# Four modulation vectors of a hybrid encoder layer: summed beside the branch merge instead of in the delta-rule stage, two of them straight into columns

## The chip, the cores and the metric

The kernel runs on one core of one Trainium2 chip. The core has five engines that run at once, each through an instruction list of its own, in order: PE (TensorE, matrix products, with its weight loads listed apart as PEld), DVE (VectorE), ACT (ScalarE), POOL (GpSimd) and SP (SyncE, which here issues nearly all DMA transfers). They wait for one another through semaphores. The metric is the device time of one execution in microseconds (us), as the median of several runs. All data is float32. Large products are made from operands split into a high part and a remainder of a reduced format ("fp32r"), three products for one.

## The reference, cut to what matters

One layer over 1024 tokens of width 1024. A conditioning vector c gives six vectors of 1024 numbers; the first two modulate the input, the last four are those of this change.

```
mod = silu(c) @ w_ada + b_ada                 # 1024 x 6144 matrix, once
shift_t, scale_t, gate_t, shift_f, scale_f, gate_f = split(mod, 6)
h = x * (1 + scale_t) + shift_t
proj = h @ w_in
o_a = gated_deltanet(...)                     # 8 heads, chunks, delta rule
o_b = chunk_band_attention(...)               # 16 heads
merged = sigmoid(gates_a) * (o_a @ w_branch_a) + sigmoid(gates_b) * (o_b @ w_branch_b)
x = layernorm(alpha * x + gate_t * (merged @ w_o), ln1_g, ln1_b)
h = x * (1 + scale_f) + shift_f
u = causal_dwconv(h @ w_up) + b
x = layernorm(alpha * x + gate_f * ((silu(u_gate) * u_val) @ w_down), ln2_g, ln2_b)
```

gate_t is needed first after the merge, shift_f and scale_f right after it in the first layer norm, gate_f only near the end.

## The kernel before, in words

The work runs through these stages; tokens lie along rows or columns of 128-wide tiles.

- **Head** (to about 95 us): the first two modulation vectors, x transposed and modulated, written as a high part `hh` and a remainder `hl`.
- **Delta-rule stage** (to about 860 us, its last chain to 920): for each of 8 heads the projections (`halves`, L281), convolutions, a triangular solve on DVE (L660, L662), an inverse by small matrix products (L684 on), and a chain over 8 chunks (L720 on). Between the heads PE is filled with projections of the merge gates (`gate_block`). Here, two calls a head, sits `mod_rows` (L800 to L823): a column block of 512 of the last four vectors is summed on DVE. Each of its four transfers brings 128 x 2 x 512 numbers (512 KB) of `w_ada` into a buffer `raw` (L808); DVE multiplies each half by a number per partition and adds it to a sum (L813 the first, L815 the other seven). PE then adds the 128 partitions with one product against a tile of ones (L819), DVE adds the bias (L822), and the row goes to `mod_d` in DRAM (L823). Eight blocks, 32 transfers, 64 DVE operations. Sum and row live in the two buffers of the ring `gt`, which the gate projections also use to store their results.
- **Attention** (about 780 to 1342 us), 16 heads. Its last heads overlap with the next stage.
- **Merge** (about 1253 to 1455 us): for branch A (`br` 0) and B (`br` 1) and each j of 8, `wblock` loads a block of 128 columns of `w_branch` into `raw`, ACT casts it to `wh` (L174), POOL takes the remainder `wl` (L177), and PE runs 48 products of 512 columns (L1039). At j = 5 to 7 of branch A, branch B's input is loaded and split the same way (ACT, DVE); in branch B the output weights `wo` are.
- **Mix** (about 1455 to 1550 us): the product with `w_o` (L1103), first layer norm, x transposed and modulated (L1155) with columns `g1f` and `b1f`. shift_f and scale_f come back from `mod_d` as 16 rows (L1110), are transposed on PE (L1112) and turned into those columns by four small DVE operations (L1116 to L1119). gate_t comes back as a broadcast tile `gtb`.
- **Up, down, last norm** (to the end).

Two things set the order around the change. First, a scheduler writes each engine's list before the run, from a simulated timeline and priorities; on the chip each engine follows its list whatever comes ready. Second, buffers are handed on in the order of the program text: `raw` has three buffers, taken in turn by every `wblock`, every split load and every `w_ada` transfer, and a transfer into one waits until the one three places earlier in the text has been used up. The slot called B4 holds, in attention, part of the transposed probabilities (the group "X", only for groups of query tiles with more than 8 blocks); after attention the group "M" lies there, from which the ring `macc` is cut.

```
    "phx": _at("X", 512, 2), "plx": _at("X", 512, 2, 256),
    ...
    group("X", _E1[4], 1024, F32R)
    ...
    group("M", _E1[4], 1024)
```

Of the kernel before, what the change touches and what calls it, by code (L numbers as in the profile page):

```python
# [9 lines left out]
F32 = mybir.dt.float32  # L10
F32R = mybir.dt.float32r
AF = mybir.ActivationFunctionType
ALU = mybir.AluOpType
# [4 lines left out]
P = 128  # L18
S = 1024
D = 1024  # L20
NK = 8
# [16 lines left out]
RB = 3  # L38
# [35 lines left out]
def _at(group, step_, n, first=0):  # L74
    return tuple((group, first + step_ * i) for i in range(n))
# [26 lines left out]
    "bt": _at("GA", 640, 2), "sb": (*_at("GA", 640, 4, 1280), ("FA", 384)),  # L102
    "ot": (("GA", 3840), ("FA", 0)), "mx": _at("FA", 4, 8, 256),

    "gb": _at("GB", 512, 2), "macc": _at("M", 0, 1), 
    "st": _at("ST", 12, 2), "mv": _at("ST", 4, 4, 36), "gtb": (_E1[0],), "g1b": (_E1[1],),
    "b1b": (_E1[2],), "r": (_E1[3], ("GL", 0)), "x1": _at("GL", 1024, 2, 1024),
    "h2": _at("GL", 0, 1, 3072),
# [42 lines left out]
def hybrid_layer(  # L151
# [69 lines left out]
    def nm(s):  # L221
        uid[0] += 1
        return f"{s}_{uid[0]}"
# [34 lines left out]
    def ring(key, shape, dtype=F32):  # L258
        return place(step(key, AT[key]), shape, dtype, key)
# [5 lines left out]
    def mtile(name, tag="m"):  # L265
        return pbank(name, tag)
# [531 lines left out]
    macc = [None]  # L798

    def mod_rows(i):  # L800

        cb = i // 2
        if i % 2 == 0:
            macc[0] = ring("gt", [P, 512])
        acc = macc[0]
        for k0 in range(4 * (i % 2), 4 * (i % 2) + 4, 2):
            rv = W.tile([P, 2, 512], F32, tag="raw", bufs=RB, name=nm("raw"))
            SP.dma_start(rv, w_ada2[k0 * P:(k0 + 2) * P,  # L808
                                    2 * D + 512 * cb:2 * D + 512 * cb + 512].rearrange(
                                        "(k p) n -> p k n", p=P))  # L810
            for k in (k0, k0 + 1):
                if k == 0:
                    DVE.tensor_scalar(acc, rv[:, 0, :], csil[:, 0:1], None, ALU.mult)  # L813
                else:
                    DVE.scalar_tensor_tensor(acc, rv[:, k - k0, :], csil[:, k:k + 1], acc,  # L815
                                             ALU.mult, ALU.add)
        if i % 2 == 1:
            pr_ = mtile(nm("pmod"), "i")
            PE.matmul(pr_, ones, acc, start=True, stop=True)  # L819
            row = ring("gt", [P, 512])[0:1, :]  # L820
            SP.dma_start(row, b_ada[:, 2 * D + 512 * cb:2 * D + 512 * cb + 512])
            DVE.tensor_tensor(row, row, pr_[0:1, :], ALU.add)  # L822
            SP.dma_start(mod_d[:, 512 * cb:512 * cb + 512], row)  # L823

    gate_block(0)
    cs = [stage_k(0)]
    gates = iter([*range(1, 2 * NK), *((i,) for i in EP)])
# [9 lines left out]
    for h in range(HA):  # L837
        ORD = "sigKq"
        for o in ORD:
            if o == "s":  # L840
                with tc.high_priority(offset=PF):
                    stage_solve(h, cs[h])
            elif o == "i":
                with tc.high_priority(offset=PI):
                    stage_inverse(h, cs[h])
            elif o == "K" and h + 1 < HA:
                with tc.issue_after(last.ins) if last else nullcontext():
                    cs.append(stage_k(h + 1))
            elif o == "g":
                some_gates(GA[h])  # L850
            elif o == "q" and h + 1 < HA:
                stage_q(h + 1, cs[h + 1])
        some_gates(GB[h])
        for i in (2 * h, 2 * h + 1):
            mod_rows(i)
        if h + 1 < HA:
            stage_vz(h + 1, cs[h + 1])
        with tc.high_priority(offset=PC):
            stage_chain(h, cs[h])
        with tc.high_priority(offset=PT):  # L860
            stage_out(h, cs[h])
        last = cs[h]["last"]
# [160 lines left out]
    for k in range(NK):  # L1023
        load_split(oahk[k], oalk[k], oa_d[k], ACT, POOL if k in OL else DVE)

    wo = []
    for br in range(2):
        if br == 1:
            mh, ml = (t_.rearrange("p k s -> p (k s)").rearrange("p (t k q) -> p t k q", t=NT, k=NK)
                      for t_ in (hh, hl))  # L1030
        rh, rl = ((oahk, oalk), (obh, obl))[br]
        for j in range(NK):
            w = wblock(kview(wbr[br], j * P, P), NK)
            for n in range(2):
                N = slice(512 * n, 512 * n + 512)
                ps = pbank(nm("pbr"), "ab"[br])
                for k in range(NK):
                    for a, r in ((w[0], rh), (w[0], rl), (w[1], rh)):
                        PE.matmul(ps, a[:, k, :], r[k][:, N],  # L1039
                                  start=(k == 0 and a is w[0] and r is rh),  # L1040
                                  stop=(k == NK - 1 and a is w[1]))
# [70 lines left out]
    PE.transpose(pmr[:, 0:16], mrow, ident[0:16, 0:16])  # L1112
    aff = cst.tile([P, 24], F32, tag="aff", name="aff")
    g1f, b1f, s1 = aff[:, 0:8], aff[:, 8:16], aff[:, 16:24]
    g1c, b1c = vt[:, VO["ln1g"]:VO["ln1g"] + 8], vt[:, VO["ln1b"]:VO["ln1b"] + 8]
    DVE.tensor_scalar(s1, pmr[:, 8:16], 1.0, None, ALU.add)  # L1116
    DVE.tensor_tensor(g1f, s1, g1c, ALU.mult)
    DVE.tensor_tensor(b1f, s1, b1c, ALU.mult)
    DVE.tensor_tensor(b1f, pmr[:, 0:8], b1f, ALU.add)  # L1119
    late, t2f = [], []  # L1120
    group("TE", "FT", 1024)
    group("TO", "B4", 1024)
# [454 lines left out]
```

## Time and profile before

| | |
|---|---|
| median of 3 runs | 2288.16 us (2286.59 to 2290.62) |
| the profiled execution | 2286.11 us |
| its span, first to last instruction | 2284.4 us |
| PE, DVE, ACT, POOL busy in the span | 94%, 71%, 45%, 34% |
| mean granted clock of PE | 0.975 |
| DMA | 220.49 MB, 97 GB/s on average |

The profile gives one execution. A group's line reads: line of the kernel, engine, operation, output and inputs by tile name, shapes, count, then busy microseconds and the mean of one in nanoseconds, then the time that the engine stood idle before these instructions and what released it. A row of the timeline reads: start, length, engine, line, operation, count, and in brackets the idle time ahead of it with its releaser. In the timeline a matrix product is shown with its modelled length; products overlap, so the pace of PE is read from one start to the next. SPq is SP's list of transfers; its lengths are those of the issue, not of the transfer.

### The profile page before, as it was taken

How to read it: one execution, taken by the hardware profiler on the slowest of the kernel's cores; microseconds unless marked ns; L12 is line 12 of the kernel's file. 1: busy time of each engine (PE TensorE's matmuls, PEld its weight loads, DVE VectorE, ACT ScalarE, POOL GpSimd, SP SyncE). 2: the span in 40 equal slices, each digit the busy share in tenths (PEclk: the TensorE clock that was granted, in tenths of full speed). 3: DMA queues.
4: the chain of work that ended last, by engine and by line, in shares of the span. 5: the costliest groups of instructions: out<-in, count | busy, mean ns of one | idle time of the engine just before them, and what ended most of it. 6: DMA issues, size and time to landing. Idle time of an engine off the chain costs nothing. (4 is left out here: it accounts for less than half of the span.)

```text
span 2284.4 us, 31690 instructions
## 1 busy us (share of the span) xinstructions
PE 2144.3 (94%) x11469; PEld 1787.2 (78%) x11469; DVE 1619.3 (71%) x3194; ACT 1026.9 (45%) x2193; POOL 772.1 (34%) x653
## 2 busy tenths in 40 slices
PE   6999999999999999999999999997999999978887
PEld 5777788777877888898897888885888888866675
DVE  8468576675757754768667434479988888789988
ACT  4645343442424335667666432244544444453322
POOL 4323233222332323233433314152100000279674
PEclk9999999999999999999999999998999999989998
DMA  9232333323333312211114333421322222333232
GB/s 280 84 108 69 106 91 106 106 72 107 99 105 107 100 41 98 63 59 49 59 55 140 103 120 106 134 93 65 102 83 83 83 84 83 111 129 111 74 111 83
DMA packets 227265, 220.49 MB, mean 97 GB/s; under 512 B 27355, under 2 KB 184468, under 8 KB 227108
## 3 DMA queue, kind: packets, MB, share of 16 engines
q1 hardware_dynamic: 227027, 218.44, 30.2%
q8 instruction: 90, 1.47, 0.3%
q14 instruction: 68, 0.55, 0.1%
q10 hardware_dynamic: 80, 0.03, 0.0%
HBM read 177.48 MB, written 47.23 MB: 98 GB/s over the span
## 5 line engine op out<-in xcount | busy, mean ns | idle before, releaser
L177 POOL TENSOR_TENSOR wl<-raw,wh 128x1024 fp32r<-128x1024 f32 x88 | 212.3, 2414 | 328.3 <-ACT wh L174 284.9
L1278 PE MATMUL pup<-hh,wop 128*128 128x512 f32 x704 | 228.8, 396 | 6.0 <-ACT SB L1291 4.0
L1278 PE MATMUL pup<-t,wop 128*128 128x512 f32 x792 | 190.1, 393 | 3.9 <-DVE t L177 2.5
L1278 PEld LDWEIGHTS pup<-t,wop 128*128 128x128 f32 x792 | 148.6, 188 | 37.9 <-DVE t L177 2.8
L1278 PEld LDWEIGHTS pup<-hh,wop 128*128 128x128 f32 x704 | 134.9, 192 | 35.7 <-ACT SB L1291 4.4
L1319 POOL TENSOR_TENSOR cc<-cc,G 128x512 f32<-128x512 f32 x22 | 36.8, 1671 | 362.5 <-DVE G L1301 313.3
L174 ACT CAST wh<-raw 128x1024 fp32r<-128x1024 f32 x88 | 92.4, 1050 | 139.5 <-DMA raw<-in_w_in_dram 55.9
L281 PE MATMUL pqkv<-hh,wh 128*128 128x512 f32 x352 | 142.8, 406 | 0.0
L281 PE MATMUL pqkv<-hl,wh 128*128 128x512 f32 x352 | 140.7, 400 | 0.0
L1278 PE MATMUL pup<-hl,wop 128*128 128x512 f32 x352 | 139.8, 397 | 0.8 <-DVE hl L177 0.8
L281 PE MATMUL pqkv<-hh,wl 128*128 128x512 f32 x352 | 139.5, 398 | 0.0
L1461 PE MATMUL pdn<-dop,dop 128*128 128x512 f32 x480 | 121.8, 412 | 18.5 <-DVE dop L177 8.6
L660 DVE TENSOR_TENSOR FT<-FT,G 128x16 f32<-128x16 f32 (+30 forms) x248 | 120.8, 487 | 18.2 <-POOL G L605 10.9
L941 POOL TENSOR_SCALAR G<-G,FT 128x640 f32<-128x640 f32 (+4 forms) x103 | 70.3, 685 | 182.3 <-DVE FT L940 161.3
L1461 PEld LDWEIGHTS pdn<-dop,dop 128*128 128x128 f32 x480 | 94.0, 198 | 43.9 <-DVE dop L177 9.7
L174 ACT CAST wop<-wr 128x512 fp32r<-128x512 f32 x110 | 67.7, 622 | 123.1 <-DVE wr L1264 71.5
L177 DVE TENSOR_TENSOR wop<-wr,wop 128x512 fp32r<-128x512 f32 x110 | 79.9, 734 | 25.8 <-ACT wop L174 25.1
L281 PE MATMUL pgt<-hh,wl 128*128 128x512 f32 x240 | 95.1, 396 | 0.8 <-POOL wl L177 0.8
L281 PE MATMUL pgt<-hh,wh 128*128 128x512 f32 x240 | 95.4, 397 | 0.1
L281 PE MATMUL pgt<-hl,wh 128*128 128x512 f32 x240 | 94.7, 395 | 0.0
L960 DVE TENSOR_TENSOR pl<-pp,ph 128x512 fp32r<-128x512 f32 (+2 forms) x116 | 72.5, 635 | 17.4 <-ACT ph L959 16.6
L1338 DVE SCALAR_TENSOR_TENSOR G<-cc,vt,G 128x1023 f32<-128x1023 f32 (+1 forms) x58 | 76.0, 1315 | 7.9 <-ACT G L1335 7.9
(487 smaller groups left out, 6297.4 us busy)
## 6 DMA issues: line engine op xcount, KB each, us to landing
raw<-in_w_in_dram SPq DMA_DIRECT2D x72, 512.0 KB
wr<-in_w_up_dram SPq DMA_DIRECT2D x44, 512.0 KB
raw<-in_w_ada_dram SPq DMA_DIRECT2D x32, 512.0 KB
wa<-in_w_ada_dram SPq DMA_DIRECT2D x32, 256.0 KB
gates_d<-GT SPq DMA_DIRECT2D x32, 256.0 KB
dr<-g_d SPq DMA_DIRECT2D x16, 512.0 KB
dr<-in_w_down_dram SPq DMA_DIRECT2D x16, 512.0 KB
g_d<-G SPq DMA_DIRECT2D x15, 512.0 KB
```

What stands on the lines that cost most here:

```text
L174: ACT.copy(h, src)
L177: return le.tensor_tensor(l, src, f(h), ALU.subtract).ins
L281: PE.matmul(ps, a[:, k, :], r[k][:, 512 * n:512 * n + 512], start=(k == 0 and a is wh and r is rh), stop=(k == NK - 1 and a is wl))
L660: DVE.tensor_tensor(pr[:, :, 0:i + 1], ft[:, :, 0:i + 1], fa[:, i:i + 1, 0:i + 1].to_broadcast([P, 8, i + 1]), ALU.mult)
L941: POOL.tensor_scalar(sb[:, 0:n], sb[:, 0:n], mx[:, 3:4], 0.0, ALU.mult, ALU.add)
L960: DVE.tensor_tensor(pl[:, B, :], pp, f(ph[:, B, :]), ALU.subtract)
L1278: PE.matmul(ps, a[:, u, k, :], b[v][k], start=(new and k == 0 and u == 0 and v == 0), stop=(k == 3 and u == 1), skip_group_check=not new)
L1319: self.later(7, lambda: POOL.tensor_tensor(o, o, self.t, ADD))
L1338: DVE.scalar_tensor_tensor(y[:, d:], cc[:, :S - d], col("conv_f", tap * 44 + ti), y[:, d:], ALU.mult, ALU.add)
L1461: PE.matmul(sets[s_][i], a[:, u, i * P:i * P + P], b[:, v, :], start=(new and j == 0 and u == 0 and v == 0), stop=(j == nq - 1 and u == 1) ...
```

## The change

The function `mod_rows` leaves the delta-rule stage. A function `mod_half` with the same transfers and the same 64 sums is called once for each of the 16 steps of the merge (two branches, eight j). Its sum lies in the ring `macc`, now two buffers in slot B4. For shift_f and scale_f (blocks 2 to 5) PE no longer makes a row: four products with the sum as weights and one column of ones give the 512 sums as four columns, DVE adds the bias from `vt` straight into `aff`, and the way through `mod_d`, the 16-row transfer and the transposition fall away. For the two gates (blocks 0, 1, 6, 7) the row is made as before, but in the sum's own buffer: the transfer of the bias into it waits for the product that reads the sum.

```
-    "gb": _at("GB", 512, 2), "macc": _at("M", 0, 1), 
+    "gb": _at("GB", 512, 2), "macc": _at("M", 512, 2), 
...
-        for i in (2 * h, 2 * h + 1):
-            mod_rows(i)
...
+    def mod_half(i):
+        cb = i // 2
+        if i % 2 == 0:
+            macc[0] = ring("macc", [P, 512])
+        acc = macc[0]
+        for k0 in range(4 * (i % 2), 4 * (i % 2) + 4, 2):
+            rv = W.tile([P, 2, 512], F32, tag="raw", bufs=RB, name=nm("raw"))
+            SP.dma_start(rv, w_ada2[...])
+            for k in (k0, k0 + 1):
+                if k == 0:
+                    DVE.tensor_scalar(acc, rv[:, 0, :], csil[:, 0:1], None, ALU.mult)
+                else:
+                    DVE.scalar_tensor_tensor(acc, rv[:, k - k0, :], csil[:, k:k + 1], acc,
+                                             ALU.mult, ALU.add)
+        if i % 2 == 0:
+            return
+        pr_ = pbank(nm("pmod"), "mod")
+        if 2 <= cb < 6:
+            for q in range(4):
+                PE.matmul(pr_[:, q:q + 1], acc[:, q * P:q * P + P], ones[:, 0:1], start=True, stop=True)
+            o, v = 8 + 4 * (cb - 2), VO["b_ada"] + 16 + 4 * cb
+            DVE.tensor_tensor(aff[:, o:o + 4], pr_[:, 0:4], vt[:, v:v + 4], ALU.add)
+        else:
+            PE.matmul(pr_, ones, acc, start=True, stop=True)
+            row = acc[0:1, :]
+            SP.dma_start(row, b_ada[:, 2 * D + 512 * cb:2 * D + 512 * cb + 512])
+            DVE.tensor_tensor(row, row, pr_[0:1, :], ALU.add)
+            SP.dma_start(mod_d[:, 512 * cb:512 * cb + 512], row)
...
+            mod_half(NK * br + j)
...
-    mrow = ring("macc", [P, P])[0:16, :]
-    SP.dma_start(mrow, mod_d[:, D:3 * D].rearrange("o (r p) -> (o r) p", p=P))
-    pmr = pbank("pmr", "t")
-    PE.transpose(pmr[:, 0:16], mrow, ident[0:16, 0:16])
```

The scheduler writes all lists anew. Three places matter here. The first is PE's list in the merge, where j = 5 of branch A ends and j = 6 begins (`pbr` is the output bank of a half block, `wh` and `wl` its weights). Before:

```order
L1039 MATMUL pbr_12790<-hh,wh_12757 128x512
L1039 MATMUL pbr_12790<-hl,wh_12757 128x512
L1039 MATMUL pbr_12790<-hh,wl_12758 128x512
L1039 MATMUL pbr_12831<-hh,wh_12825 128x512
L1039 MATMUL pbr_12831<-hl,wh_12825 128x512
L1039 MATMUL pbr_12831<-hh,wl_12826 128x512
```

And now, with the same end of j = 5 (`pmod` is the bank of the modulation's sums):

```order
L1046 MATMUL pbr_12673<-hl,wh_12640 128x512
L1046 MATMUL pbr_12673<-hh,wl_12641 128x512
L1027 MATMUL pmod_12426<-B_1554_12234,ones 128x512
L1027 MATMUL pmod_12567<-B_1554_12234,ones 128x512
L1023 MATMUL pmod_12708<-ones,B_1554_12234 128x1 x4
L1046 MATMUL pbr_12728<-hh,wh_12722 128x512
L1046 MATMUL pbr_12728<-hl,wh_12722 128x512
L1046 MATMUL pbr_12755<-hh,wh_12722 128x512
L1046 MATMUL pbr_12755<-hl,wh_12722 128x512
L1046 MATMUL pbr_12728<-hh,wl_12723 128x512
```

Between j = 5 and j = 6 the products of the first three blocks now stand in a row; then come four products of j = 6 that need `wh` alone, and then the first with `wl`. The last head of attention has its last product 32 rows ahead of the first `pmod`.

The second place is SP's list there. Before, the weights of j = 6 and 7 (`raw_12827`, `raw_12899`, from `w_branch_a`) and of the first step of branch B stand among branch B's input loads:

```order
L1043 DMA ma_12412<-gates_d 128x512 x2
L182 DMA raw_12821<-ob_d 128x1024
L182 DMA raw_12827<-in_w_branch_a_dram 128x8x128
L182 DMA raw_12899<-in_w_branch_a_dram 128x8x128
L182 DMA raw_12893<-ob_d 128x1024
L182 DMA raw_12961<-ob_d 128x1024
L182 DMA raw_13037<-in_w_branch_b_dram 128x8x128
```

Now the weights of j = 6 are `raw_12724`:

```order
L1029 DMA B_1554_12234<-in_b_ada_dram 1x512
L1009 DMA raw_12559<-in_w_ada_dram 128x2x512
L1031 DMA mod_d<-B_1554_12234 1x512
L1009 DMA raw_12563<-in_w_ada_dram 128x2x512
L1009 DMA raw_12632<-in_w_ada_dram 128x2x512
L1009 DMA raw_12636<-in_w_ada_dram 128x2x512
L1009 DMA raw_12700<-in_w_ada_dram 128x2x512
L1029 DMA B_1554_12234<-in_b_ada_dram 1x512
L1009 DMA raw_12704<-in_w_ada_dram 128x2x512
L1031 DMA mod_d<-B_1554_12234 1x512
L182 DMA raw_12718<-ob_d 128x1024
L182 DMA raw_12724<-in_w_branch_a_dram 128x8x128
```

They stand behind all twelve `w_ada` transfers of blocks 0 to 2; the first six of these (`raw_12350`, `raw_12354`, `raw_12418`, `raw_12422`, `raw_12491`, `raw_12495`) are further up in the list. By the turns of the ring, one of the three buffers carries `raw_12354`, `raw_12422`, `raw_12495`, `raw_12563`, `raw_12636`, `raw_12704` and then `raw_12724`, each after the one before it has been used; a second carries the other six.

The third place is DVE's list at the end of attention (`B_812` is slot B4 with attention's probabilities, `B_1554` the same slot with the new sums, `ma` the merge's first branch, `ob` attention's output). Before:

```order
L960 TENSOR_TENSOR B_852_7310<-pp_12380,B_852_7310 128x256
L177 TENSOR_TENSOR G_12401<-raw_12961,G_12401 128x1024
L1045 SCALAR_TENSOR_TENSOR ma_12410<-ma_12410,pbr_12763 128x512
L177 TENSOR_TENSOR ob_12420<-raw_12821,ob_12414 128x1024
L977 TENSOR_TENSOR ob_12023<-po_12385,FT_7309 64x256
```

Now:

```order
L931 TENSOR_TENSOR B_812_7142<-pp_12212,B_812_7142 128x256
L1052 SCALAR_TENSOR_TENSOR ma_12241<-ma_12241,pbr_12605 128x512
L1014 TENSOR_SCALAR B_1554_12234<-raw_12350,csil 128x512
L1016 SCALAR_TENSOR_TENSOR B_1554_12234<-raw_12350,csil,B_1554_12234 128x512
L948 TENSOR_TENSOR ob_11855<-po_12217,FT_7141 64x256
L1016 SCALAR_TENSOR_TENSOR B_1554_12234<-raw_12354,csil,B_1554_12234 128x512 x2
L1052 SCALAR_TENSOR_TENSOR ma_12242<-ma_12242,pbr_12646 128x512
L1016 SCALAR_TENSOR_TENSOR B_1554_12234<-raw_12418,csil,B_1554_12234 128x512 x2
```

The first sum stands behind the last write of attention into slot B4, and it waits for PE, which reads that slot last.

More of the change, by code (lines that the diff above doesn't have):

```diff
@@ L796, in gate_block @@
             SP.dma_start(gates_d[j][:, N], gt_)
[L798 to L823, printed above, removed]
     gate_block(0)
@@ L1024, in hybrid_layer @@
         load_split(oahk[k], oalk[k], oa_d[k], ACT, POOL if k in OL else DVE)
+    aff = cst.tile([P, 24], F32, tag="aff", name="aff")
+    macc = [None]
+    def mod_half(i):
[5 more added lines that the diff above has]
+            rv = W.tile([P, 2, 512], F32, tag="raw", bufs=RB, name=nm("raw"))
+            SP.dma_start(rv, w_ada2[k0 * P:(k0 + 2) * P,
+                                    2 * D + 512 * cb:2 * D + 512 * cb + 512].rearrange(
+                                        "(k p) n -> p k n", p=P))
+            for k in (k0, k0 + 1):
[18 more added lines that the diff above has]
+            SP.dma_start(mod_d[:, 512 * cb:512 * cb + 512], row)
     wo = []
@@ L1108, in hybrid_layer @@
     ps, nxt = mix(0), mix(1)
-    mrow = ring("macc", [P, P])[0:16, :]
-    SP.dma_start(mrow, mod_d[:, D:3 * D].rearrange("o (r p) -> (o r) p", p=P))
-    pmr = pbank("pmr", "t")
-    PE.transpose(pmr[:, 0:16], mrow, ident[0:16, 0:16])
-    aff = cst.tile([P, 24], F32, tag="aff", name="aff")
-    g1f, b1f, s1 = aff[:, 0:8], aff[:, 8:16], aff[:, 16:24]
+    b1f, s1, g1f = aff[:, 8:16], aff[:, 16:24], aff[:, 0:8]
     g1c, b1c = vt[:, VO["ln1g"]:VO["ln1g"] + 8], vt[:, VO["ln1b"]:VO["ln1b"] + 8]
-    DVE.tensor_scalar(s1, pmr[:, 8:16], 1.0, None, ALU.add)
+    DVE.tensor_scalar(s1, s1, 1.0, None, ALU.add)
+    DVE.tensor_tensor(g1f, s1, b1c, ALU.mult)
+    DVE.tensor_tensor(b1f, b1f, g1f, ALU.add)
     DVE.tensor_tensor(g1f, s1, g1c, ALU.mult)
-    DVE.tensor_tensor(b1f, s1, b1c, ALU.mult)
-    DVE.tensor_tensor(b1f, pmr[:, 0:8], b1f, ALU.add)
     late, t2f = [], []
```

## The prediction

> **What bounds the kernel now.** I read the page first, then the busy times by stage, then PE's waits. The first line of the page says that PE is the engine to watch; the table by stage (columns: stretch, its length, busy time of PE, PEld, DVE, ACT, POOL with their instruction counts, PE's clock, DMA) shows where it is filled and where not.
>
> ```profile
> PE 2144.3 (94%) x11469; PEld 1787.2 (78%) x11469; DVE 1619.3 (71%) x3194; ACT 1026.9 (45%) x2193; POOL 772.1 (34%) x653
> ```
>
> ```profile
> 95.00:860.00 765.00, 733.88 (x4437) 608.77 (x4436) 510.37 (x1277) 307.16 (x849) 223.75 (x221) 0.99 0.32 95
> 1205.00:1342.00 137.00, 132.12 (x731) 113.18 (x730) 79.25 (x211) 73.31 (x146) 50.16 (x47) 0.96 0.36 117
> 1342.00:1460.00 118.00, 118.00 (x520) 97.28 (x519) 46.87 (x49) 29.07 (x36) 39.57 (x24) 1.00 0.40 129
> 1460.00:1550.00 90.00, 90.00 (x421) 73.92 (x420) 63.97 (x90) 29.66 (x62) 37.21 (x20) 1.00 0.33 112
> 1550.00:1640.00 90.00, 75.75 (x300) 59.71 (x300) 80.56 (x113) 46.29 (x78) 14.82 (x8) 0.91 0.21 68
> ```
>
> The delta-rule stage (first row) leaves PE idle for 765 - 733.9 = 31.1 us, with DVE busy for two thirds. The rest of the merge after attention (third row) leaves PE no idle time at all, at full clock, while DVE has 71 us free. So work taken from DVE in the first stage can only shorten PE's 31.1 us, and work put into the merge is free only as long as PE never waits for it: every wait there adds to the time in full.
>
> **What goes from the delta-rule stage.** On DVE, 64 sums and 8 bias additions, 43.3 + 3.9 + 5.4 = 52.6 us; and DVE stood 15.6 us in front of L813, because the sum's buffer still held a gate result that was being stored.
>
> ```profile
> L815 DVE SCALAR_TENSOR_TENSOR GT<-raw,csil,GT 128x512 f32<-128x512 f32 x56 | 43.3, 774 | 3.6 <-DMA raw<-in_w_ada_dram 2.3
> ...
> L822 DVE TENSOR_TENSOR GT<-GT,pmod 1x512 f32<-1x512 f32 x8 | 5.4, 672 | 3.7 <-PE pmod L819 3.7
> ...
> L813 DVE TENSOR_SCALAR GT<-raw,csil 128x512 f32<-128x512 f32 x8 | 3.9, 484 | 19.6 <-DMA gates_d<-GT 15.6 <-DMA qk_d<-GT 4.0
> ```
>
> What of that PE feels is in its waits of that stage (who waited <- for whom: us, times, longest):
>
> ```profile
> PE pxt L684 <- DMA G<-ft_d: 9.4, 10, 2.3
> PE pvn L726 <- DVE vs L723: 6.5, 8, 2.6
> ```
>
> The first is for the end of the solve, which is DVE's work followed by a small transfer, the second for a step of the chain on DVE: 15.9 us that shorter queues on DVE can shorten, of the 31.1. Most of each is latency of the chain itself, so I take a third, 5 us. The ends: 31.1 if DVE were behind all of it, and -5 if the new order in that stage happens to place as much anew. On PE, eight products against the ones leave. The next two rows are PE's timeline: from the start of one such pair to the next product are 265.50 - 264.64 = 0.86 us, eight times 6.9 us, on the path since PE is filled.
>
> ```profile
> 264.64 1.02 PE L819 MATMUL pmod<-GT,ones 128*128 128x512 f32 x2
> 265.50 0.38 PE L722 MATMUL pks<-SA,y 128*128 128x128 f32 x2
> ```
>
> Gain in the delta-rule stage: 6.9 + 5 = 11.9 us. SP's 32 transfers and 16 small ones go from a queue that nothing in those waits names; I cost that at nothing.
>
> **What comes into the merge: PE's products.** Four gate blocks at 0.86 us. The column form is in the trace at L394 (two products of that form are the four records):
>
> ```profile
> 29.31 0.50 PE L394 MATMUL pmods<-ones,G 128*128 128x1 f32 x4
> 29.67 0.47 PE L281 MATMUL pfirst<-hl,wh 128*128 128x512 f32 x1
> ```
>
> 29.67 - 29.31 = 0.36 us for two, so about 0.8 us (a little over 0.72 for the change of form) for a block's four. The transposition that goes is one product of 231 ns:
>
> ```profile
> L1112 PE MATMUL pmr<-ident,B 16*128 16x16 f32 x1 | 0.2, 231 | 0.0
> ```
>
> **What comes into the merge: a chain.** This is the step that decides. The sums lie in slot B4, which attention's last head reads on PE; DVE's list has the first sum behind that, and PE's list has blocks 0, 1 and 2 ahead of all of j = 6. So PE must wait until twelve transfers have gone through two `raw` buffers, and then until the weights of j = 6, next in one of these buffers, have been loaded. The rows for each step: PE at the end of attention and its pace, a `w_ada` transfer from issue to use on an otherwise quiet queue (SP, then DVE), and the same with two in flight.
>
> ```profile
> 1340.48 0.28 PE L971 MATMUL po<-B,v 128*64 128x256 f32 x1
> 1341.58 0.44 PE L1039 MATMUL pbr<-hh,wh 128*128 128x512 f32 x1
> 1342.10 0.39 PE L1039 MATMUL pbr<-hh,wl 128*128 128x512 f32 x1
> 1342.33 0.39 PE L1039 MATMUL pbr<-hh,wh 128*128 128x512 f32 x1
> ```
>
> ```profile
> 161.23 0.38 SPq L808 DMA_DIRECT2D raw<-in_w_ada_dram  x1
> ```
>
> ```profile
> 165.80 1.54 DVE L815 SCALAR_TENSOR_TENSOR GT<-raw,csil,GT 128x512 f32<-128x512 f32 x2 [0.64 <-DMA raw<-in_w_ada_dram]
> ...
> 766.25 2.32 DVE L815 SCALAR_TENSOR_TENSOR GT<-raw,csil,GT 128x512 f32<-128x512 f32 x3 [1.68 <-DMA raw<-in_w_ada_dram]
> ```
>
> ```profile
> L808 SPq DMA_DIRECT2D raw<-in_w_ada_dram x32: 367/384/1717, 124.0 to 761.0; - x32
> ```
>
> A load takes 165.80 - 161.23 = 4.57 us to its use, the last one (761.0, two in flight) 5.25; I take 4.57, since in the chain the two buffers are half a turn apart, and keep 5.25 as the upper end. The two sums on a buffer take 1.54. For the weights and for the inputs of branch B: the load of 512 KB from `ob_d` (SP, then ACT), the casts, the remainders on POOL and DVE, and one small DVE step of attention:
>
> ```profile
> 1343.95 0.33 SPq L182 DMA_DIRECT2D raw<-ob_d  x1
> ```
>
> ```profile
> 1348.15 1.05 ACT L174 CAST ob<-raw 128x1024 fp32r<-128x1024 f32 x1 [5.09 <-DMA raw<-ob_d]
> ```
>
> ```profile
> L174 ACT CAST wh<-raw 128x1024 fp32r<-128x1024 f32 x8 | 8.4, 1052 | 22.6 <-PE pbr L1039 12.1 <-DMA raw<-in_w_branch_b_dram 10.5
> L177 POOL TENSOR_TENSOR wl<-raw,wh 128x1024 fp32r<-128x1024 f32 x8 | 19.2, 2398 | 28.8 <-DMA raw<-in_w_o_dram 20.9 <-ACT wh L174 7.8
> ```
>
> ```profile
> L177 DVE TENSOR_TENSOR ob<-raw,ob 128x1024 fp32r<-128x1024 f32 x6 | 7.3, 1223 | 7.6 <-ACT ob L174 4.7 <-DMA ob_d<-ob 2.9
> L977 DVE TENSOR_TENSOR ob<-po,FT 64x256 f32<-64x256 f32 x9 | 3.8, 423 | 3.3 <-ACT FT L976 3.1
> ```
>
> Zero is the last read of slot B4 (1340.48 in the trace of before). PE then has 1.1 us of attention and 32 products at 0.23: done at 8.5. On the buffer that the weights need:
>
> - first two buffers' sums, already loaded, and the step of attention between them: 0.48 + 0.77 + 0.42 + 1.54 = 3.2;
> - five refills of 4.57 + 1.54 = 6.1: 33.7; one more us for the row additions in between (0.67 each, partly hidden): 34.7;
> - weights of j = 6: load 4.57, cast 1.05: `wh` at 40.3; POOL 2.40: `wl` at 42.7.
>
> PE does four products at 40.3 and the rest from 42.7, instead of from 8.5 on: 42.7 - 8.5 - 0.9 = **33.3 us** of delay; the first three blocks' products hide in it. Then the same buffer turns on: an `ob_d` load (4.2 + 1.05 + 1.22 = 6.5), then weights (4.57 + 1.05 + 2.40 = 8.0). `wl` of j = 7 is there at 57.2, PE ready for it at 53.3 (44 products, then two with `wh`): 3.9. First step of branch B: 71.7 against 69.5 (46 products, 0.8 for block 3, four with `wh`): 2.2. After that weights follow weights on this buffer, 8.0 a turn against PE's 48 products of 11 us: none. Together 39.4.
>
> Outside of the waits, products of five blocks: 3 x 0.8 + 2 x 0.86 - 0.2 = 3.9. And the clock: after a wait PE resumes slower. The row of 1550 to 1640 has 14.25 us of idle PE and a clock of 0.91, 8.1 us lost over idle and working time together; 0 to 8, I take 2. The merge: 39.4 + 3.9 + 2 = **45.3 us**.
>
> In the mix, gate_t's last transfer is due long before its use; SP's wait for block 7's product stands ahead of one `wo` load, whose end comes no later than before by the list. DVE's 53 us of sums fit into its free 71.
>
> The Trainium skill, "DMA: Bandwidth & Descriptors", Anatomy of one DMA, fits a transfer as 2.0 us plus bytes over 436 GB/s, for a GpSimd-issued one: 3.2 us as an estimate for 512 KB, against 4.57 in the row. By it the eight loads in these waits would take 11 us less, and the time would be 2310.6. These transfers are issued by SP, and the rows of this case decide.
>
> **Sum.** 45.3 - 11.9 = +33.4 us. Against the profiled execution (2286.11: span 2284.4 and 1.7 around it) that is 2319.5; the median of the runs stands 2.05 higher, so the forecast is 2321.6.
>
> **The rivals.**
>
> - *The buffer is free early* (faster). If the first sum is released by an earlier head than the last, the three blocks run beside attention; the transfers are in `raw` long before, and no product waits. Then the merge costs 4 x 0.86 + 4 x 0.8 - 0.2 = 6.4, and the time is 2288.2 - 11.9 + 6.4 = 2282.7. It decides once the slot is free 40 us before attention ends. Against it: the first sum stands behind attention's last write into that slot. 0.07.
> - *DVE was behind all of PE's idle time in the delta-rule stage* (no change). The gain is then 31.1 + 6.9 = 38.0; with loads at the 4.2 us of the `ob_d` row (8 x 0.4 = 3) and no loss of clock, the merge costs 40.3: 2290.5. Against it: casts on ACT and transfers are behind part of those waits. 0.05.
> - *Absorbed later.* PE's 14.25 idle us after 1550 shrink, because DVE gains time in the long wait: 2321.6 - 14.3 = 2307.3. Against it: what DVE does after 1550 depends on the mix. 0.10.
> - *More waits in branch B.* A ring that carries `wo` loads as well may cost five more steps 2.2 us each: 2332.6. For it: three buffers carry 7 loads per two steps. 0.16.
>
> **How the numbers follow.** My forecast has 0.62. Its own ends: the loads at 4.2 (-3), no clock loss (-2), all 15.9 us of waits gained (-10.9): 2305.7; loads at 5.25 (+5.4), clock 8 (+6), no wait gained (+5): 2338.0. With absorption and more waits inside, the range is 2303 to 2338. A difference of 0.2% (4.6 us) is about what a measurement here tells from none. Slower is the forecast with absorption and more waits, 0.62 + 0.10 + 0.16 = 0.88; same 0.05; faster 0.07.
>
> The Trainium skill, "TensorE: Matmul & The Clock Gate", Part 1, says that one idle window of about 3.4 us halves PE's clock until a busy one has passed; as an estimate a resumption loses 1.7 us or a little more. No row here separates that.
>
> **What would show it.** In the profile after: a gap on PE of some 30 us (less the three blocks) about 10 us after attention's last product, with a lower digit of the clock beside it; two or three `L1009` transfers at a time in SP's timeline, each behind a DVE sum; `pbr` released by ACT's `wh` or POOL's `wl` at j = 6, 7 and 8. In the delta-rule stage, PE's two waits smaller and the stage 7 to 23 us shorter. I am wrong if PE stays filled from 1342 on, or if the stage before has grown.

## The result and the profile after

The kernel after takes 2320.73 us in the median of 4 runs (2314.71 to 2323.31), the kernel before 2288.1; the ratio is 1.0136, 95% interval 1.012 to 1.0153. The forecast was 2321.6. The total came out within a microsecond, but two of its terms were each wrong by more than that, and the errors cancelled. The profiled run is the fastest of the four (2314.71 us, mean granted clock 0.974; the others lie between 2320.63 and 2323.31, at 0.967 to 0.971), so the profile shows a loss of 28.5 us between the spans (2312.9 and 2284.4) where the medians show 32.6.

The page and the stretches of the kernel after, cut at the same times as the prediction's table (columns: stretch, length, busy PE, PEld, DVE, ACT, POOL, PE's clock, DMA share, GB/s):

```profile
PE 2146.2 (93%) x11492; PEld 1784.2 (77%) x11492; DVE 1616.5 (70%) x3194; ACT 1030.6 (45%) x2195; POOL 769.8 (33%) x653
```

```profile
95.00:860.00 765.00, 742.11 (x4535) 619.11 (x4534) 470.14 (x1239) 320.95 (x882) 224.66 (x228) 1.00 0.26 75
...
1205.00:1342.00 137.00, 116.08 (x616) 96.81 (x614) 75.01 (x181) 55.91 (x113) 39.28 (x34) 0.91 0.40 129
1342.00:1460.00 118.00, 102.86 (x438) 82.85 (x439) 64.70 (x82) 25.63 (x29) 37.00 (x20) 0.92 0.59 188
1460.00:1550.00 90.00, 83.99 (x377) 67.54 (x376) 56.51 (x73) 27.39 (x51) 31.03 (x18) 1.00 0.45 151
...
```

The delta-rule stage has become fuller (PE's idle time 22.9 us instead of 31.1), and the merge, which had none, now has holes. The hole that the prediction described is in PE's timeline. These are the last read of slot B4 (the prediction's zero), the last product of j = 5, the products of blocks 0, 1 and 2 with the idle time ahead of them, and the first products of j = 6 with `wh` and with `wl`:

```profile
1313.92 0.28 PE L942 MATMUL po<-B,v 128*64 128x256 f32 x1
...
1322.12 0.39 PE L1046 MATMUL pbr<-hh,wl 128*128 128x512 f32 x1
1325.87 1.38 PE L1027 MATMUL pmod<-B,ones 128*128 128x512 f32 x2 [3.37 <-DVE B L1016]
1337.04 2.05 PE L1027 MATMUL pmod<-B,ones 128*128 128x512 f32 x2 [9.79 <-DVE B L1016]
1348.22 1.84 PE L1023 MATMUL pmod<-ones,B 128*128 128x1 f32 x8 [9.13 <-DVE B L1016]
1352.55 0.80 PE L1046 MATMUL pbr<-hh,wh 128*128 128x512 f32 x1 [2.49 <-ACT wh L174]
...
1355.00 0.79 PE L1046 MATMUL pbr<-hh,wl 128*128 128x512 f32 x1 [0.38 <-POOL wl L177]
```

The links of the chain, on DVE (the first sum, waiting for attention's product), SP (the issue of the weights of j = 6), ACT and POOL:

```profile
1314.24 0.49 DVE L1014 TENSOR_SCALAR B<-raw,csil 128x512 f32<-128x512 f32 x1 [3.18 <-PE po L942]
```

```profile
1348.10 0.38 SPq L182 DMA_DIRECT2D raw<-in_w_branch_a_dram  x1
```

```profile
1351.45 1.04 ACT L174 CAST wh<-raw 128x1024 fp32r<-128x1024 f32 x1 [2.13 <-DMA raw<-in_w_branch_a_dram]
```

```profile
1352.58 2.37 POOL L177 TENSOR_TENSOR wl<-raw,wh 128x1024 fp32r<-128x1024 f32 x1 [59.89 <-ACT wh L174]
```

Counted from 1313.92: the first sum starts at 0.3, PE has done its work at 8.6, the weights are issued at 34.2, PE uses `wh` at 38.6 and `wl` at 41.1. The prediction had 0, 8.5, 34.7, 40.3 and 42.7. POOL's 59.89 us of idle time say the same from another side: no weights came.

### The profile page after: what moved, and what is told of

Same layout as the page of the kernel before. It is cut to its first block, busy times and chain, and to the rows that moved or that the text cites. A ratio compares the mean times of both kernels' runs of the same rounds, so it can differ in the third digit from the quotient of the medians.

```text
span 2312.9 us, 31767 instructions
## 1 busy us (share of the span) xinstructions
PE 2146.2 (93%) x11492; PEld 1784.2 (77%) x11492; DVE 1616.5 (70%) x3194; ACT 1030.6 (45%) x2195; POOL 769.8 (33%) x653
## 5 line engine op out<-in xcount | busy, mean ns | idle before, releaser
L1281 PEld LDWEIGHTS pup<-hh,wop 128*128 128x128 f32 x704 | 134.6, 191 | 34.7 <-ACT SB L1294 4.4
L177 DVE TENSOR_TENSOR wop<-wr,wop 128x512 fp32r<-128x512 f32 x110 | 80.1, 735 | 24.2 <-ACT wop L174 24.1
```

The lines of the kernel that those rows point to most:

```text
L177: return le.tensor_tensor(l, src, f(h), ALU.subtract).ins
L1281: PE.matmul(ps, a[:, u, k, :], b[v][k], start=(new and k == 0 and u == 0 and v == 0), stop=(k == 3 and u == 1), skip_group_check=not new)
```

## The experiments

All times are medians; "before" beside them is the kernel before, measured next to the run on the same chip. First a table, then each run.

| run | what | us | before | ratio (95%) |
|---|---|---|---|---|
| 1 | after, sums in slot A5 | 2314.64 | 2288.28 | 1.0119 (1.0102 to 1.0136) |
| 2 | before, blocks left out | 2271.19 | 2288.28 | 0.9925 (0.9909 to 0.9942) |
| 3 | before, transfers left out | 2308.40 | 2288.28 | 1.0092 (1.0077 to 1.0107) |
| 4 | before, sums left out | 2291.62 | 2288.28 | 1.0016 (1.0005 to 1.0027) |
| 5 | run 1, and another bank | 2299.79 | 2288.31 | 1.0049 (1.0034 to 1.0064) |
| 6 | 128-column blocks in attention | 2349.75 | 2288.31 | 1.0278 (1.0254 to 1.0301) |
| 7 | 128-column blocks in the delta-rule stage | 2371.84 | 2288.31 | 1.0359 (1.0337 to 1.0380) |
| 8 | before, shift and scale as columns | 2280.12 | 2288.31 | 0.9970 (0.9956 to 0.9984) |
| 9 | before, all eight as columns | 2290.05 | 2287.90 | 1.0013 (1.0003 to 1.0023) |
| 10 | after, all transfers left out | 2272.91 | 2287.90 | 0.9934 (0.9920 to 0.9949) |
| 11 | after, 12 transfers left out | 2296.69 | 2287.17 | 1.0039 (1.0025 to 1.0053) |

**Runs 1 and 5: is it the slot?** The theory: the sums begin only when attention's last head has read slot B4, and the weights of j = 6 stand behind their transfers. The rival: whatever the slot, three transfer buffers are too few for twelve more loads.

```
-MA = (_E1[5], _E1[6], _E0[1], _E0[3], _E0[5], "GT", "SA", "SB")
+MA = (_E1[5], _E1[6], _E0[1], _E0[3], "GT", "SA", "SB", _E1[4])
...
-    group("M", _E1[4], 1024)
+    group("M", _E0[5], 1024)
...
-    group("TO", "B4", 1024)
+    group("TO", "A5", 1024)
```

> The kernel after, with the sums in slot A5 (last read by the 14th head of attention) instead of B4 (last read by the 16th); A5's place among the buffers of branch A is taken by the next slot, and B4 becomes the buffer of j = 7, which is loaded last. Theory of the prediction (the first sum waits for the last head's read of B4, and the weights of j = 6 stand behind all twelve transfers in their buffer): the sums run beside the last two heads, the wait of about 30 us on PE between j = 5 and j = 6 shrinks to a few us, the smaller waits of branch B stay; 2320.7 - 30 = about 2291, range 2280 to 2297. Rival (the twelve transfers hold up the weights in the buffer ring whatever slot the sums lie in, since 512 KB loads and sums of 6.1 us a turn are the limit): the wait keeps over 20 us, 2311 or more. Rival (it is the products of the sums in PE's order that cost): no change, 2318 to 2323.

Measured: 2314.64, so the expectation failed. The sums did move; DVE's timeline of this run has the first at 1233 and the one that ends block 1 at 1264:

```profile
1233.37 1.81 DVE L1014 TENSOR_SCALAR A<-raw,csil 128x512 f32<-128x512 f32 x1
...
1263.79 0.81 DVE L1016 SCALAR_TENSOR_TENSOR A<-raw,csil,A 128x512 f32<-128x512 f32 x1
...
1334.70 0.68 DVE L1030 TENSOR_TENSOR A<-A,pmod 1x512 f32<-1x512 f32 x1 [1.66 <-DMA A<-in_b_ada_dram]
1336.66 0.48 DVE L1014 TENSOR_SCALAR A<-raw,csil 128x512 f32<-128x512 f32 x1 [1.28 <-DMA mod_d<-A]
```

After the sum at 1263.79 DVE has none for 70 us. PE's timeline of the run shows why: the product of block 0 still stands behind attention's last product, and with two sum buffers, block 2 waits until the row of block 0 has left.

```profile
1332.15 1.02 PE L1027 MATMUL pmod<-A,ones 128*128 128x512 f32 x2
1335.43 1.79 PE L1027 MATMUL pmod<-A,ones 128*128 128x512 f32 x2 [2.26 <-DVE A L1030]
1346.39 1.84 PE L1023 MATMUL pmod<-ones,A 128*128 128x1 f32 x8 [9.17 <-DVE A L1016]
1351.96 0.80 PE L1046 MATMUL pbr<-hh,wh 128*128 128x512 f32 x1 [3.73 <-ACT wh L174]
```

The products' result lies in bank 7 (ring `mod`), and that is also attention's output bank (ring `po`); banks are handed on in text order like buffers. Run 5 adds one edit:

```
-        pr_ = pbank(nm("pmod"), "mod")
+        pr_ = pbank(nm("pmod"), "a" if i < NK else "mod")
```

> The run with the sums in slot A5, and in branch A the bank for the sums' products is taken from branch A's own two banks instead of the one in which attention sums its output. In the run with slot A5 alone the sums of blocks 0 and 1 were done 70 us before attention ended, but their products still stood behind attention's last product on PE, since they had to wait for its bank, and block 2 could only begin when the row of block 0 had left; PE's wait between j = 5 and 6 was still 19.7 us. Theory (two resources in a row, the slot and then the bank, keep the chain behind attention, and the weights of j = 6 stand behind it in their buffer): now the wait goes, 2314.6 - 20 = about 2295, range 2286 to 2300. Rival (the ring of three transfer buffers is too slow for twelve more loads, wherever the products stand): over 2308.

Measured: 2299.79, as expected. PE's timeline of this run has block 2's product at 1336.83, 12 us after attention's last product (1324.86), and behind it the first product of j = 6 with 1.70 us of idle time ahead:

```profile
1336.83 0.95 PE L1023 MATMUL pmod<-ones,A 128*128 128x1 f32 x8
...
1339.47 0.50 PE L1046 MATMUL pbr<-hh,wh 128*128 128x512 f32 x1 [1.70 <-DVE ma L1052]
```

So two resources held the chain, the slot and the bank, both until attention's end, and freeing one showed the other. The rival falls: the same twelve loads go through the same three buffers, spread over attention's last heads, without the long wait. Run 5 is still slower than before: the sums now run between attention's own steps on DVE, and branch B's waits remain (both are sized below).

**Runs 10 and 11: what do the transfers cost?** Sums, products, slot and bank as in the kernel after; the transfers are left out, of all blocks or of blocks 0 to 2, and the sums read a tile of ones.

```
-            rv = W.tile([P, 2, 512], F32, tag="raw", bufs=RB, name=nm("raw"))
-            SP.dma_start(rv, w_ada2[...])
+            rv = ones[:, 0:1].unsqueeze(2).to_broadcast([P, 2, 512])
```

> The kernel after with the 32 transfers of w_ada left out: the sums read a tile of ones instead (so the four vectors have other values); slot B4, the 64 sums, the products and the rows stay in the merge. Theory (the merge's loss comes from the ring of three buffers: 24 sums can wait for attention's last head if no weights stand behind their transfers): the merge costs its products and little else, 2271.2 + 6.4 = about 2278, range 2274 to 2286. Rival (DVE's 50 us of sums and the products' places on PE cost in the merge by themselves): the greater part of the loss stays, 2300 or more.

> The kernel after with the transfers of blocks 0 to 2 alone left out (their sums read a tile of ones, so gate_t and the first half of shift_f have other values); the 20 transfers of blocks 3 to 7, all sums and products stay. It apportions the 47.8 us that all 32 transfers cost. Theory (12 transfers ahead of the weights of j = 6 make the long wait of 30 us, the other 20 make small waits of their own in the rest of the merge): 2320.7 - 30 = about 2291, range 2286 to 2297. Rival (the small waits are the tail of the long one, three buffers can carry the other 20 transfers beside PE): 2273 to 2281.

Measured: 2272.91, a little below the theory's range, and 2296.69, inside it. The rest of the merge in run 10 leaves PE no idle time, at full clock, with all of DVE's sums in it:

```profile
1325.00:1445.00 120.00, 120.00 (x541) 98.32 (x541) 97.89 (x119) 27.40 (x34) 41.91 (x23) 1.00 0.35 112
```

Without its transfers the change would gain 15 us. All 32 cost 2320.73 - 2272.91 = 47.8 us: the 12 ahead of j = 6 cost 24.0, the other 20 cost 23.8. One reservation: without the transfers the scheduler also put the products of blocks 0 to 2 later on PE, and in run 11 it moved the first products of the mix up to 1383.5, into branch B, so both shares hold for transfers and places together. What it is about the transfers that costs, the three buffers, their places in SP's list or the rate of the DMA engines, no run separates; none has a fourth buffer.

**Runs 2, 3 and 4: what does the delta-rule stage give back?** All three are the kernel before. Run 2 leaves `mod_rows` out (the bias is copied into the rows), run 3 its transfers (the sums read `hh`), run 4 the sums (for each transfer one operation of two columns is left, for each block one copy).

```
+    SP.dma_start(mod_d[:, :], b_ada[:, 2 * D:6 * D])
...
-        for i in (2 * h, 2 * h + 1):
-            mod_rows(i)
```

```
-            rv = W.tile([P, 2, 512], F32, tag="raw", bufs=RB, name=nm("raw"))
-            SP.dma_start(rv, w_ada2[...])
+            rv = f(hh[:, k0:k0 + 2, 0:512])
```

```
+        if i % 2 == 0:
+            DVE.tensor_copy(acc[:, 8:512], f(hh[:, 0, 8:512]))
...
-            for k in (k0, k0 + 1):
...
+            DVE.tensor_scalar(acc[:, k0:k0 + 2], rv[:, :, 0], csil[:, 0:1], None, ALU.mult)
```

> The kernel before with the eight blocks left out of the delta-rule stage: no transfers of w_ada for them, no sums, no products; the bias alone is copied into the rows, so the last four vectors lack their product with the matrix. It measures what the delta-rule stage gives back when the work goes. The prediction said 6.9 + 5 = 11.9 us: 2276. The two traces show PE's work of that stage ending 22.7 us earlier in the kernel after: by them about 2265, range 2260 to 2270.

> The kernel before with the 32 transfers of w_ada left out of the delta-rule stage; the 64 sums, the products and the rows stay, the sums read numbers that lie in SBUF (so the four vectors have other values). If DVE's time and PE's products cost the stage its 23 us, this is like the kernel before: 2285 to 2290. If it is the transfers (their share of the ring of three buffers, of SP and of DMA) that make the weights of the projections late: 8 to 16 us less, 2272 to 2280.

> The kernel before with the 32 transfers, the products and the rows kept, but the 64 sums of 128 x 512 replaced by one operation of two numbers a partition for each transfer and one copy a block (so the four vectors have other values). If DVE's sums are behind PE's waits and the lower clock: 2288 - (23 - 6.9) = 2272, range 2268 to 2276. If the transfers are: 2283 to 2289. If it is the rows (one transfer of the bias and one store a block, for which DVE waits at the ring of gate results): 2283 to 2289 too, but the waits name that ring.

Measured: 2271.19, 2308.40 and 2291.62. Run 2: the stage gives back 17.1 us, more than the predicted 11.9 and less than the 22.7 that the two profiled runs had suggested. Run 3 was to be between no change and a gain, and lost 20 us; run 4 was to gain 16 or nothing, and lost 3, which is within the 0.2%. The parts do not add up, so none of the offered causes is right by itself. Each edit makes the scheduler write other lists for the whole stage; that these move PE's waits by more than the removed work does is the likely reason, argued and not shown. PE's waits of run 3 between 95 and 870 us, and its sums on DVE:

```profile
PE pvn L726 <- DVE vs L723: 17.6, 13, 4.6
...
PE pxt L684 <- DMA G<-ft_d: 7.7, 7, 2.9
```

```profile
L812 DVE SCALAR_TENSOR_TENSOR GT<-hh,csil,GT 128x512 f32<-128x512 f32 x56 | 55.6, 993 | 1.3
```

The wait for the chain's step on DVE is 17.6 us, against 6.5 before. The sums are as many as before, but they take 55.6 us instead of 43.3 (the last section shows why), so run 3 does not leave DVE's time as it was, and its loss is not that of a new order alone.

**Runs 6 and 7: the same work in small pieces.** 32 blocks of 128 columns; one transfer each, eight sums in place in the transfer's buffer, one product of one column; no sum slot, no row. Run 6 calls it after each head of attention, run 7 in the delta-rule stage.

```
+    def mod_col(q, bank):
+        rv = W.tile([P, NK, P], F32, tag="raw", bufs=RB, name=nm("raw"))
+        SP.dma_start(rv, kview(w_ada2, 2 * D + P * q, P))
+        acc = rv[:, 0, :]
+        DVE.tensor_scalar(acc, acc, csil[:, 0:1], None, ALU.mult)
+        for k in range(1, NK):
+            DVE.scalar_tensor_tensor(acc, rv[:, k, :], csil[:, k:k + 1], acc, ALU.mult, ALU.add)
+        pr_ = pbank(nm("pmod"), bank)
+        PE.matmul(pr_[:, 0:1], acc, ones[:, 0:1], start=True, stop=True)
```

> The four vectors in another form and place: 32 blocks of 128 columns, each one transfer of 512 KB, eight sums in place in the transfer's buffer, one product with a column of ones and one addition into a column; no sum buffer, no row; two blocks after each head of attention. The gates' columns are stored to DRAM once a gate. Theory (the delta-rule stage gives back 17 us, as in the run without the blocks, and the work costs nothing if it neither waits for a slot nor stands ahead of the weights): 2271.2 + 4 us of products + 0 to 10 of disturbed attention: 2275 to 2285. Rival (DVE's 50 us cost attention as much as they cost the delta-rule stage, since DVE stands in its chain of each head): 2286 to 2300.

> The same form of 32 blocks of 128 columns, left in the delta-rule stage, four blocks a head. It separates the place from the form. If it is DVE's and the transfers' time that cost the delta-rule stage its 17 us, only the products' share comes back (32 small ones for 8 of 0.86 us, 3 to 4 us): 2282 to 2287. If it is the rows and the sums in the two buffers of gate results, 10 us or more come back: 2272 to 2279.

Measured: 2349.75 and 2371.84, far outside. The size of DVE's operations was overlooked. In run 6 the 224 sums take 108.2 us, where the kernel before needs 43.3 for the same numbers in 56 operations of 512 columns:

```profile
L806 DVE SCALAR_TENSOR_TENSOR raw<-raw,csil 128x128 f32<-128x128 f32 x224 | 108.2, 494 | 2.2
```

In run 7 they take 116.8 us. That is 73.5 us more than before on an engine that stands in the chains of the stage, and the time rose by 83.5. That DVE's time counts in the delta-rule stage when it grows is the likely reading, not a shown one: in this form a transfer's buffer is also held for eight sums instead of two, and between 95 and 860 us PE waited 7.8 us in run 7 for weights of the projections (`pqkv` behind ACT's `wh`), a wait that the kernel before does not have there. Run 4 shows that taking DVE's time away gives nothing by itself.

**Runs 8 and 9: a part of the change alone.** Run 8 is the kernel before with blocks 2 to 5 as columns straight into `aff` (so their rows, the 16-row transfer and the transposition fall away), all in the delta-rule stage; run 9 does the same with the gates, whose columns go to DRAM once a gate.

```
+            if 2 <= cb < 6:
+                for q in range(4):
+                    PE.matmul(pr_[:, q:q + 1], acc[:, q * P:q * P + P], ones[:, 0:1], start=True, stop=True)
+                o, v = 8 + 4 * (cb - 2), VO["b_ada"] + 16 + 4 * cb
+                DVE.tensor_tensor(aff[:, o:o + 4], pr_[:, 0:4], vt[:, v:v + 4], ALU.add)
+                return
```

> One part of the change alone: the kernel before with blocks 2 to 5 (shift and scale) as columns, four products of one column into aff, no row, no transposition; everything stays in the delta-rule stage, the gates as rows. By the prediction's terms: 4 x (0.86 - 0.8) + 0.2 = 0.4 us of PE and 2.7 us of DVE's row additions less: 2284 to 2289. A new order of the stage's lists could move it by 10 us either way, which would show in PE's waits there and not in the removed operations.

> The run with shift and scale as columns in the delta-rule stage was 8 us faster than before. Here all eight blocks are columns there: the gates too have four products of one column each, no row, no second turn in the two buffers of gate results; the gates' columns are stored to DRAM once a gate. Theory (the rows and their turns in the ring of gate results were behind that gain): the other four rows bring about as much again, 2272 to 2278. Rival (the gain came with the new order of the lists alone): no further gain, 2278 to 2290, either way of the run before it.

Measured: 2280.12, faster than both kernels (0.9970, 0.9956 to 0.9984), and 2290.05, no change by the 0.2% bound. With four more rows gone the gain was gone too, so fewer rows do not bring it by themselves. The execution in run 8's trace took 2284.15 us, half of the way back to the kernel before, so the trace does not show where the 8 us lie; that stays open. It is the best complete version found; whether a new order of the lists or a part of the change is behind it, no run shows.

## Why the prediction was right in its total, point by point

**The chain in the merge: right in mechanism and nearly in size.** Released by attention's last read, twelve transfers, then the weights: every link came within 1.7 us. The first three blocks' products hid in the wait, as said. What the prediction did not see is that the slot was one of two locks. Its rival "the buffer is free early" was priced at 2282.7 and decided "once the slot is free 40 us before attention ends". In run 1 the sums began some 90 us before attention's end (1233.4, its last product at 1326.3), and the gain was 6 us; the bank was the second lock, and with both open it was 2299.79, still 17 above that price. In that run's trace the first six steps of branch A, between attention's last heads, took 102.7 us instead of 92.8, and branch B, to the start of the mix, took 97.0 instead of 87.4.

**The later waits in the merge: too small.** The next rows are the first products of branch B and of the mix, before and after (first and last start at the end):

```profile
L1039 PEld LDWEIGHTS pbr<-ob,wh x192: 187/188/188, 1367.3 to 1452.9; 128*128 128x128 f32 x192
```

```profile
L1103 PEld LDWEIGHTS pwo<-wo,hh x256: 186/188/192, 1454.7 to 1548.3; 128*128 128x128 f32 x128
```

```profile
L1046 PEld LDWEIGHTS pbr<-ob,wh x192: 186/188/330, 1379.2 to 1477.4; 128*128 128x128 f32 x192
```

```profile
L1111 PEld LDWEIGHTS pwo<-wo,hh x256: 186/188/193, 1481.0 to 1578.3; 128*128 128x128 f32 x128
```

Branch B begins 65.3 us after the zero, where before it began 26.8 after it (1367.3 - 1340.48): 38.5 later. Of these, 3.3 are products of j = 5 that were still to do (next point), so 35.2 belong to the merge; the prediction had 33.3 + 3.9 of waits up to here and 0.8 of products, 38.0. From there to the mix it is 101.8 us instead of 87.4, 14.4 more; the prediction had 2.2 of wait, 3.1 of products and 2 of clock, 7.3. The mix takes 97.3 instead of 93.6, 3.7 more, predicted as nothing. Together 53.3 against 45.3. The cause is the rival "more waits in branch B", which came true beside the forecast and not instead of it. PE's waits from 1357 to 1500 us:

```profile
PE pbr L1046 <- POOL wl L177: 4.1, 4, 1.4
PE pbr L1046 <- DVE FT L1054: 3.8, 2, 2.0
PE pwo L1111 <- DVE wo L177: 2.6, 1, 2.6
PE pmod L1027 <- DVE B L1016: 0.9, 1, 0.9
```

Of the first row 0.9 us belong to j = 7; so in branch B PE waits 7.9 us, where the prediction had 2.2, and in the mix 2.6 for `wo`. Run 10, which has the same sums without transfers, has none of these waits. The failed step is "After that weights follow weights on this buffer ... none" and, for the mix, "whose end comes no later than before by the list". Run 11 points the same way from the other side: the 20 transfers of the later blocks cost 23.8 us.

**The gain ahead of the merge: too small.** The prediction had 6.9 of products and 5 of waits. From rows: attention's last read of B4 comes 1340.48 - 1313.92 = 26.6 us earlier, of which PE pays 3.3 back at once (8.6 us of branch A's j = 5 are left to do instead of 5.2, from 1340.48 to the first product of j = 6 here):

```profile
1345.73 0.39 PE L1039 MATMUL pbr<-hh,wh 128*128 128x512 f32 x1
```

So 23.3 in the profiled runs, and 17.1 by run 2's medians. The two waits that the prediction named gave 3.8 us:

```profile
PE pxt L684 <- DMA G<-ft_d: 6.8, 8, 2.1
PE pvn L726 <- DVE vs L723: 5.3, 10, 0.8
```

All of PE's idle time in the stage fell by 8.2. The term that was missing altogether is the clock. In these five stretches of 45 us the kernel before, and then the kernel after, had:

```profile
140.00:185.00 45.00, 40.53 (x217) 33.21 (x216) 34.57 (x85) 19.22 (x44) 9.54 (x12) 0.92 0.43 124
410.00:455.00 45.00, 41.10 (x277) 33.46 (x276) 28.83 (x67) 17.20 (x46) 11.71 (x17) 0.96 0.41 118
500.00:545.00 45.00, 41.94 (x226) 34.12 (x226) 27.84 (x73) 19.79 (x48) 9.61 (x12) 0.96 0.26 82
770.00:815.00 45.00, 42.38 (x280) 39.08 (x279) 37.64 (x109) 17.15 (x65) 13.55 (x8) 0.96 0.20 56
815.00:860.00 45.00, 42.30 (x315) 35.59 (x314) 17.66 (x45) 13.48 (x37) 12.89 (x22) 0.96 0.25 74
```

```profile
140.00:185.00 45.00, 42.90 (x231) 34.50 (x229) 29.96 (x70) 20.08 (x45) 9.90 (x13) 0.96 0.24 71
410.00:455.00 45.00, 42.40 (x294) 34.20 (x293) 23.76 (x59) 15.79 (x46) 12.56 (x19) 1.00 0.22 65
500.00:545.00 45.00, 43.16 (x286) 35.02 (x285) 19.04 (x43) 15.14 (x38) 13.28 (x18) 1.00 0.30 88
770.00:815.00 45.00, 44.93 (x347) 41.23 (x347) 25.62 (x80) 12.95 (x48) 9.86 (x13) 1.00 0.07 18
815.00:860.00 45.00, 41.84 (x264) 34.68 (x263) 22.81 (x64) 21.27 (x53) 11.99 (x18) 1.00 0.29 90
```

The others stand at 1.00 in both. The loss by clock is the sum of 45 x (1 - clock): 10.8 us before, 1.8 after, 9.0 less. 6.9 + 8.2 + 9.0 = 24.1, against the 22.6 by which the last `pxt` product came earlier:

```profile
L684 PEld LDWEIGHTS pxt<-G,am x256: 106/113/158, 171.6 to 839.8; 128*32 128x32 f32 x128
```

```profile
L684 PEld LDWEIGHTS pxt<-G,am x256: 106/113/158, 166.0 to 817.2; 128*32 128x32 f32 x128
```

The sum is rough: a slow clock during idle time costs nothing, and the stretch up to 860 us holds more of the later work in the kernel after. And part of the 22.6 is luck of one execution or of one list. In the traces of runs 11, 1, 10, 5 and 2, whose delta-rule stage holds no blocks either, the same product starts at 818.9, 819.7, 822.0, 822.4 and 823.8, which is 16.0 to 20.9 earlier than before; the kernel after has the largest gain of the six. How much of this spread is the clock and how much the lists was not tried.

**The sum.** In the profiled run: 53.3 - 23.3 = 30.0, which is what the rows have at the end of the mix (1578.3 - 1548.3); both terms were too small, by 8.0 and by 11.4. At the end of the spans 28.5 are left, so the rival "absorbed later" gave 1.5 us of its 14.3. In the medians, with run 2's gain of 17.1 and a time 32.6 above before, the loss is some 49.7 against 45.3: errors of 5.2 and 4.4 that cancel. The forecast's place in the middle of its range is partly luck; its sign and its mechanism are not.

## What to carry to other kernels

Before work is put under a filled engine, list every resource that it shares with the stage it should hide in: the slot it writes, the bank of its result, the ring that its transfers go through, each handed on in text order. Opening one lock shows the next, and the transfers, not the arithmetic, were what this change paid for (15 us of gain without them, 33 of loss with them). And in a stage whose order a scheduler writes anew, what removing work is worth cannot be read off the work alone: here the whole piece gave 17 us, and one part of it cost 20.

## What the runs showed of the hardware that was not expected

A DVE operation of two SBUF inputs can stand still for as long as a POOL operation runs. In run 7 the sums of 128 columns have a median of 351 ns but a mean of 523; the longest take 2785. DVE's and POOL's timelines of the same stretch:

```profile
306.90 2.44 DVE L806 SCALAR_TENSOR_TENSOR raw<-raw,csil 128x128 f32<-128x128 f32 x1
309.26 0.68 DVE L623 TENSOR_TENSOR at<-pkq,tmp 128x512 f32<-128x512 f32 x1
309.87 4.21 DVE L806 SCALAR_TENSOR_TENSOR raw<-raw,csil 128x128 f32<-128x128 f32 x2
```

```profile
306.82 4.75 POOL L177 TENSOR_TENSOR wl<-raw,wh 128x1024 fp32r<-128x1024 f32 x2 [2.49 <-ACT wh L174]
...
311.59 2.34 POOL L633 TENSOR_TENSOR y<-y,tmp 128x1024 f32<-128x1024 f32 x1
```

The sum that starts 0.08 us after POOL's first remainder ends only when that has ended; the operation between, whose first input is in PSUM, ran at its 0.68 us beside POOL. The Trainium skill, "SBUF — State Buffer", section Who interferes with whom, says that a DVE instruction with two SBUF inputs contends with a POOL instruction that reads SBUF, over a pair of ports that only one of the two can hold at a time; these rows agree. Of run 7's 224 sums 22 are longer than 1 us, and each of them ends 0.15 us after the end of a TENSOR_TENSOR on POOL; they hold all of the 224 x (523 - 351) ns = 38.5 us by which the sums exceed their median. The 56 sums of the kernel before lose 56 x (774 - 751) ns = 1.3 us (their median is 751). The number of operations is not all of it: the 56 sums of run 3 (median 752) lose 56 x (993 - 752) ns = 13.5 us, in seven operations that each end 0.55 us after one of POOL's remainders `wl`.

PE's clock can fall to half for a few microseconds behind waits that are shorter than the fall. In the delta-rule stage of the kernel before PE waits 2.40 us up to 501.61 and 0.72 up to 503.46, and no longer wait stands nearby; then the clock is 0.50 for 3.4 us, and the products of 512 columns, which start 0.23 us apart before and after, start 0.43 apart (504.80, 505.23, 505.65):

```profile
502.90:506.30 3.40, 2.84 (x9) 2.46 (x10) 2.85 (x10) 2.02 (x5) 0.00 (x0) 0.50 0.12 45
```

The longest single wait of PE in that stage is 2.6 us, so all of its 10.8 us of lost clock come with waits of that size or smaller.
